# Hybrid attention block: softmax sums divided out of y^T, residual rows loaded early, six z tiles computed as Strassen pairs between the gate pairs

## The chip, the cores and the metric

The kernel runs on one core of a Trainium2 chip. The core has a matrix engine (TensorE, PE in the profile, with PEld for its weight loads), three engines for elementwise work (VectorE, DVE; ScalarE, ACT; GpSimd, POOL) and a sync engine whose queue (SP) issues all DMAs here. PE writes to PSUM, eight banks of 128 x 512 fp32. The metric is the device time of one execution in microseconds.

## The reference

One decoder block on x of 1024 rows by 1024 channels, all fp32:

```python
h = rms_norm(x, g_pre)
qa, ka, va, fa, za, qb, kb, vb, zb, gates = split(h @ w_in)
ya = fox_attention(qa, ka, va, log_sigmoid(fa + b_forget))      # 8 heads of 64, causal
ya = ya * silu(za)
yb = (softmax(q1 k1^T) - lam * softmax(q2 k2^T)) @ vb           # 4 heads of 128, rope on q, k
yb = rms_norm(yb, g_subln) * (1 - lam_init) * silu(zb)
ga, gb = split(sigmoid(gates))
merged = ga * (ya @ w_branch[0]) + gb * (yb @ w_branch[1])
out = x + rms_norm(merged @ w_out, g_post)
```

The two z projections (za and zb) together have 1024 columns: eight tiles of 128 columns, z tile 0 to 3 from za and 4 to 7 from zb. The gates have 2048 columns: eight tiles d for each of the two branches.

## The kernel before

**Arithmetic.** Every fp32 operand of a product is split into a high part and a low part (fp32r), and a product is the sum of three matmuls: high x high, high x low, low x high. A projection of one tile of 128 columns on 1024 rows, with 8 blocks of the inner dimension, is 2 row halves x 8 x 3 = 48 matmuls of 512 columns (`project`, L242 to 248). The normed input lies transposed in SBUF as hT, indexed by part (high or low), inner half kh and row half sh.

**Order.** The program is written as a sequence; a scheduler places each engine's instructions in a fixed order at compile time. Its stages are:

1. Normalize x, transpose it into hT, compute the values V (L119 to 222).
2. Attention, units u = 0 to 7 (L251 to 645). Units 0 to 3 are a differential head each, 4 to 7 two forgetting heads each. A unit's rows come in groups of two row blocks of 128. `s_row` (L410 to 431) makes one row block of softmax: scores on PE (L421, L422), bias, scale and row extreme on DVE (L423), exp on ACT with the row sum accumulated into `le` (L428), and 1/le on DVE (L430). A differential row scales p2 by -lambda/l2 on POOL (L512), p1 by 1/l1 on ACT (L514) and adds them on POOL (L515); a forgetting row is scaled by 1/l on POOL (L542). `av` (L433 to 483) then transposes the rows on PE, splits them into high and low (ACT L453, DVE L454) and multiplies with V (L474). y^T is stored to DRAM (y_d). Between the groups stand filler tasks (L623 to 644): the k and q projections of the next unit (`unit_proj`; for a differential unit with rope, whose half swaps are DMAs, L287), the z tiles that ZFILL gives to the unit (`z_tasks`, which store the projection to z_d), the sums of hT for the later Strassen products (`h_combinations`, TFILL), and the squares of y for the sub-norm (`sum_squares`, `subln_scales`, SFILL), which leave the row factors in rs_d.
3. Gates (L747 to 821). Tile d = 0 plain, d = 1 to 7 in pairs: the two branches' tiles as one 2 x 2 block product by Winograd's form of Strassen's method, seven products of 12 matmuls in place of eight (`wino`, L697 to 740; `left_operands`, L669 to 695). The sums of the weights run on POOL (L677), the splits on ACT (L664) and DVE or POOL (L665), the sums of the products on DVE (L706). The results pass a sigmoid on ACT and go to DRAM (g_d). After pair d stand the blocks `y_work(t, c)` that YORD[d] names (L762 to 772): y_t times the sub-norm factor (t < 4), times z, times sigmoid(z); z comes back from z_d. Weights for a pair are loaded into two buffers with the tag wraw; work tiles of 512 columns come from `tmp`, tag t, 8 buffers.
4. Branch products (L824 to 873): y^T is split (yT, L837, L838) into slots that the gate stage has used, then 384 matmuls (L848) and the merge with the gates into mg.
5. Output product (L876 to 970), again by Strassen pairs: `out_pair(i)` makes row blocks i and i + 4 from mg. `out_half` loads the residual half row (L931), squares (ACT, L933), multiplies by g_post (DVE L936 or POOL L939), and, when both halves of a row are there, forms the row factor on POOL (L943, L112, L113) and applies it and the residual (L948 to L951) before the store (L952). The residual tile `ox` has two buffers.

Of the kernel before, what the change touches and what calls it, by code (L numbers as in the profile page):

```python
# [46 lines left out]
def tile_hybrid_block(  # L47
# [47 lines left out]
    sub_rs = const.tile([P, 4, 8], F32, name="sub_rs")  # L95

# [8 lines left out]
    ss_d = dram.tile([4, S], F32, name="ss_d")  # L105
    rs_d = dram.tile([4, S], F32, name="rs_d")
# [144 lines left out]
    with ExitStack() as st:  # L251
# [158 lines left out]
        def s_row(T, m, i, X, bias, boff, nm):  # L410
# [16 lines left out]
            le = small.tile([P, 1], F32, tag="l", name=f"l{nm}_{m}_{i}", bufs=8)  # L427
            nc.scalar.activation(pr[:, 0:n], pr[:, 0:n], AF.Exp,  # L428
                                 bias=mx[:, len(pcs) - 1:len(pcs)], scale=-1.0, accum_out=le)
            nc.vector.reciprocal(le, le)  # L430
            return pr, le
# [53 lines left out]
        def unit_attn(u, T):  # L485
# [17 lines left out]
            if diff:  # L503
                def row(i, rows):
# [3 lines left out]
                    p1, l1 = s_row(T, 0, i, rows["X"][0], dmask, boff, f"d{u}")  # L508
                    p2, l2 = s_row(T, 1, i, rows["X"][1], dmask, boff, f"d{u}")
# [4 lines left out]
                    nc.scalar.activation(p1[:, 0:n], p1[:, 0:n], AF.Copy, scale=l1)  # L514
# [17 lines left out]
            else:  # L532
                ysb = {}

                def row(m, i, rows):
# [3 lines left out]
                    if "X" not in rows:  # L539
                        rows["X"] = swapped(T, m, i // 2, f"f{u}")  # L540
                    p1, l1 = s_row(T, m, i, rows["X"], cb[m], 0, f"f{u}")
                    nc.gpsimd.tensor_scalar(  # L542
                        p1[:, 0:n], p1[:, 0:n], l1, 1.0, op0=ALU.mult, op1=ALU.mult)
                    rows[i] = p1
# [73 lines left out]
        for u in range(8):  # L618
# [4 lines left out]
            fill = []  # L623
# [5 lines left out]
            fill[2:2] = [lambda k=k: h_combinations(k) for k in TFILL[u]]  # L629
# [15 lines left out]
        pend()  # L645

# [368 lines left out]
```

## Time and profile before

| | us |
|---|---|
| median of 3 runs | 960.3 (960.2 to 962.56) |
| the profiled execution's own time | 960.13 |
| its span in the profile | 958.0 |
| DVE busy | 627.2 |
| ACT busy | 437.0 |
| POOL busy | 489.6 |

The span is what the instructions cover; the execution's own time is 2.1 us longer. Times in a trace count from the span's start. A group's row gives the line, the engine, the operation, the tiles written and read, the count, and then busy time, mean length and the idle time of the engine before these instructions, with what released it. The chain of work that ended last is followed back from the last instruction, so an engine can be busy without being on it. Matmuls are pipelined: their printed lengths overlap, and what one costs is read from how far apart they start.

### The profile page before, as it was taken

The page shows a single profiled execution, that of the slowest core. Times are in us where ns is not written, and L with a number is a line of the kernel's source. Part 1 is how long each engine was busy: PE and PEld are TensorE (multiplying, and loading weights), DVE is VectorE, ACT ScalarE, POOL GpSimd, SP SyncE. Part 2 cuts the span into 40 slices and gives each one's busy share as a digit, 9 for nine tenths or more (in the row PEclk, how much of TensorE's full clock was granted, in tenths as well). Part 3 has the DMA queues.
Part 4 walks back from the last instruction along what each step waited for, and adds up shares of the span by engine and source line. Part 5 has one row for each costly group of instructions (what it writes and reads, how often), then busy time and mean ns, then how long its engine had stood idle before and what let it go on. Part 6 is the DMA issues. An engine that isn't in the chain of part 4 may idle for free.

```text
span 958.0 us, 13760 instructions
## 1 busy us (share of the span) xinstructions
PE 900.7 (94%) x4600; PEld 752.1 (79%) x4600; DVE 627.2 (65%) x1180; ACT 437.0 (46%) x862; POOL 489.6 (51%) x460
## 2 busy tenths in 40 slices
PE   7999989899999999999999988999999999999992
PEld 5999867787887888888878877777888768887871
DVE  7731258978768868578676478228665782559875
ACT  3521125665656574565745658323443550324331
POOL 7200035446545466464644575216655735878972
PEclk9999999999999999999999999998999989999997
DMA  9532454434334353534434350893445696210144
GB/s 314 193 110 91 142 134 114 105 80 123 97 94 138 95 155 116 154 122 130 143 123 136 103 186 28 325 377 122 139 138 172 186 370 203 73 38 1 48 150 154
DMA packets 115656, 136.95 MB, mean 143 GB/s; under 512 B 10609, under 2 KB 80241, under 8 KB 114562
## 3 DMA queue, kind: packets, MB, share of 16 engines
q1 hardware_dynamic: 115586, 136.08, 44.4%
q8 instruction: 36, 0.59, 0.3%
q14 instruction: 34, 0.28, 0.1%
HBM read 85.65 MB, written 37.81 MB: 129 GB/s over the span
## 4 chain that ended last, share of the span: by engine, by line
PE 58%; DVE 13%; POOL 8%; DMA 7%; issue 6%; ACT 5%; SPq 2%; DVEq 0%; POOLq 0%; ACTq 0%
PE x_g L713 11%; PE pv L195 9%; PE pb L848 9%; PE pz L246 7%; PE pk L246 4%; PE pq L246 3%; PE ypf L474 3%; PE pg L246 2%; PE ptf L450 2%; DMA swk<-rawk 2%; SPq L287 1%; DVE Pd L423 1%; PE ypd L474 1%; PE Sf L421 1%; DVE wo_op L890 1%
## 5 line engine op out<-in xcount | busy, mean ns | idle before, releaser
L195 PE MATMUL pv<-wvhi,hT 128*128 128x264 f32 (+2 forms) x384 | 89.3, 325 | 0.4 <-DVE hT L181 0.4
L246 PE MATMUL pk<-hT,hi_k 128*128 128x512 f32 x256 | 83.9, 401 | 4.2 <-DVE KB L298 2.4
L246 PE MATMUL pz<-hT,hi_z 128*128 128x512 f32 x256 | 85.1, 400 | 0.0
L848 PE MATMUL pb<-yT,hi_br 128*128 128x512 f32 x256 | 80.8, 398 | 1.9 <-ACT hi_br L232 1.6
L246 PE MATMUL pq<-hT,hi_q 128*128 128x512 f32 x256 | 82.3, 395 | 0.0
L713 PE MATMUL x_g<-T,a_g 128*128 128x512 f32 x336 | 79.5, 392 | 1.6 <-ACT a_g L664 1.2
L713 PE MATMUL x_o<-wo_op,a_o 128*128 128x512 f32 x336 | 77.4, 391 | 2.4 <-ACT a_o L664 1.2
L713 PEld LDWEIGHTS x_o<-wo_op,a_o 128*128 128x128 f32 x336 | 62.8, 188 | 16.9 <-ACT a_o L664 2.1
L713 PEld LDWEIGHTS x_g<-T,a_g 128*128 128x128 f32 x336 | 63.5, 190 | 15.7 <-ACT a_g L664 1.6
L195 PEld LDWEIGHTS pv<-wvhi,hT 128*128 128x128 f32 x384 | 64.6, 190 | 6.2 <-DVE hT L181 0.7
L542 POOL TENSOR_SCALAR Pf<-Pf,lf 128x1024 f32<-128x1024 f32 (+3 forms) x64 | 52.5, 824 | 30.2 <-DVE lf L430 27.4
L713 PE MATMUL x_g<-hT,a_g 128*128 128x512 f32 x252 | 62.0, 400 | 2.6 <-ACT a_g L664 2.0
L428 ACT ACTIVATE Pf<-Pf,mxf 128x1024 f32<-128x1024 f32 (+3 forms) x64 | 49.8, 778 | 32.1 <-DVE mxf L423 29.5
L428 ACT ACTIVATE Pd<-Pd,mxd 128x128 f32<-128x128 f32 (+7 forms) x64 | 49.5, 774 | 30.0 <-DVE mxd L423 28.2
L538 POOL TENSOR_TENSOR cb<-cb,trim 128x128 f32<-128x128 f32 x64 | 30.0, 470 | 62.9 <-DVE mxf L423 45.1
L195 PE MATMUL pv<-wvlo,hT 128*128 128x512 f32 (+2 forms) x192 | 61.9, 325 | 0.0
L512 POOL TENSOR_SCALAR Pd<-Pd,ld 128x128 f32<-128x128 f32 (+7 forms) x32 | 25.6, 799 | 68.8 <-DVE ld L511 38.2
L848 PEld LDWEIGHTS pb<-yT,hi_br 128*128 128x128 f32 x256 | 49.1, 193 | 13.1 <-ACT hi_br L232 2.0
L713 PEld LDWEIGHTS x_g<-hT,a_g 128*128 128x128 f32 x252 | 48.5, 193 | 13.7 <-ACT a_g L664 2.4
L246 PEld LDWEIGHTS pk<-hT,hi_k 128*128 128x128 f32 x256 | 47.6, 190 | 14.4 <-DVE KB L298 2.5
L454 DVE TENSOR_TENSOR plf<-ptf,phf 128x512 fp32r<-128x512 f32 (+1 forms) x80 | 49.6, 633 | 10.1 <-ACT phf L453 9.5
L246 PEld LDWEIGHTS pz<-hT,hi_z 128*128 128x128 f32 x256 | 47.9, 191 | 8.7
(243 smaller groups left out, 2426.6 us busy)
## 6 DMA issues: line engine op xcount, KB each, us to landing
t_d<-t SPq DMA_DIRECT2D x32, 256.0 KB, 2.2
T<-t_d SPq DMA_DIRECT2D x8, 1024.0 KB, 14.9
raw<-in_w_in_dram SPq DMA_DIRECT2D x14, 512.0 KB, 4.1
g_d<-c_g SPq DMA_DIRECT2D x21, 256.0 KB, 3.9
vb_d<-vbs SPq DMA_DIRECT2D x8, 512.0 KB
va_d<-vas SPq DMA_DIRECT2D x8, 512.0 KB, 3.8
raw_k<-in_w_in_dram SPq DMA_DIRECT2D x8, 512.0 KB, 5.3
raw_q<-in_w_in_dram SPq DMA_DIRECT2D x8, 512.0 KB
```

The source lines that it names most:

```text
L195: nc.tensor.matmul(ps[n], lhsT=hT[hp][k // 4][i // 4][:, k % 4, hs], rhs=wt[k][:, a:b], start=first, stop=(k == KT - 1 and hp == 1))
L246: nc.tensor.matmul(ps, lhsT=a[:, k, :], rhs=hT[h][k // 4][c][:, k % 4, :], start=(k == 0 and a is hi and h == 0), stop=(k == KT - 1 and a ...
L287: nc.sync.dma_start(sw[b * 32:(b + 1) * 32, :], raw[o * 32:(o + 1) * 32, :])
L428: nc.scalar.activation(pr[:, 0:n], pr[:, 0:n], AF.Exp, bias=mx[:, len(pcs) - 1:len(pcs)], scale=-1.0, accum_out=le)
L450: nc.tensor.transpose(pt[:, o * P:(o + 1) * P], rows[2 * g + r][:, j * P:(j + 1) * P], ident)
L454: nc.vector.tensor_tensor(pl[:, 0:n], pt[:, 0:n], ph[:, 0:n], op=ALU.subtract)
L474: nc.tensor.matmul(o, lhsT=a, rhs=b[:, src], start=(j == 0 and n == 0), stop=(odd == 1 and jj == g and n == len(prods) - 1))
L512: nc.gpsimd.tensor_scalar(p2[:, 0:n], p2[:, 0:n], l2, 1.0, op0=ALU.mult, op1=ALU.mult)
L538: nc.gpsimd.tensor_tensor(diag, diag, trim, op=ALU.add)
L542: nc.gpsimd.tensor_scalar(p1[:, 0:n], p1[:, 0:n], l1, 1.0, op0=ALU.mult, op1=ALU.mult)
L713: nc.tensor.matmul(x[m], lhsT=a[:, ai, k, :], rhs=right[m][bi][k], start=(k == 0 and n == 0), stop=(k == 3 and n == 2))
L848: nc.tensor.matmul(ps, lhsT=a[:, kk, :], rhs=yT[g][h][:, k % 2, sl], start=(k == 0 and a is hi and h == 0), stop=(k == 3 and a is lo))
```

## The change

- **Sums out of the rows.** The row sums are kept in a tile `lsum` and no longer divided out row by row. A forgetting row goes unscaled into the product with V. A differential row is p1 + p2 x (l1 x -lambda / l2), so it is l1 times what it was. `save_sums(u)`, a filler task of unit u + 1 (after the last unit for u = 7), transposes the sums of a unit and stores them to l_d, as 1/l for the forgetting heads and as l1 for the differential ones. The sub-norm cancels l1, with the small constant scaled by l1 squared; for the forgetting heads `y_work` multiplies y^T by 1/l, loaded from l_d as a broadcast row.
- **z tiles 0 to 5** leave the filler of the units. They are computed as three Strassen pairs (0, 1), (2, 3) and (4, 5), after the gate pairs 1, 3 and 5, and each block that comes out goes straight into `y_work` as z; z_d is used for tiles 6 and 7 alone. YORD keeps four blocks of y (t = 2 and 3). All eight y tiles are loaded ahead of gate pair 1.
- **Output.** The residual rows 2, 6, 3 and 7 are loaded, after the first two output pairs, into columns of mg that those pairs have read. The last pair's order of products is (1, 6, 5, 7, 3, 4, 2) in place of (1, 6, 5, 2, 3, 7, 4). The row factor is (sum + D x eps) to the power -1/2, with g_post scaled by sqrt(D) once; one POOL operation leaves the chain of a row.

The diff, cut to its core:

```diff
-YORD = ((), ((0, 0),), ((0, 1), (1, 0)), ((1, 1), (2, 0)), ((2, 1), (4, 0), (4, 1)),
-        ((3, 0), (5, 0), (5, 1)), ((3, 1), (6, 0), (6, 1), (7, 0), (7, 1)), ())
-ZFILL = ((0,), (1,), (), (2,), (3,), (4,), (5,), (6, 7))
+ZFILL = ((), (), (), (), (), (), (), (6, 7))
+ZPAIRS = {1: 0, 3: 2, 5: 4}
+YORD = ((), (), ((2, 0),), (), ((2, 1), (3, 0)), (), ((3, 1),), ())
...
         def subln_scales(t):
-            rs = sub_rs[:, t]
+            rs, ls = sub_rs[:, t], sub_l[:, t]
             nc.sync.dma_start(rs, ss_d[t].rearrange("(p j) -> p j", j=8))
-            rstd_of(rs, rs, P, SUB_EPS)
+            nc.sync.dma_start(ls, l_d[8 + t].rearrange("(p j) -> p j", j=8))
+            nc.gpsimd.tensor_tensor(ls, ls, ls, op=ALU.mult)
+            nc.vector.scalar_tensor_tensor(rs, ls, P * SUB_EPS, rs, op0=ALU.mult, op1=ALU.add)
+            rstd_of(rs, rs, P, 0.0)
...
+        def save_sums(u):
+
+            hs = slice(8 + u, 9 + u) if u < 4 else slice(2 * u - 8, 2 * u - 6)
+            n = 8 * (hs.stop - hs.start)
+            src = lsum[:, hs].rearrange("p h i -> p (h i)")
+            if u >= 4:
+                nc.vector.reciprocal(src, src)
+            ps = pj.tile([P, CH], F32, tag="pj", name=f"pl{u}")[0:n, 0:P]
+            nc.tensor.transpose(ps, src, ident)
+            rows = small.tile([16, P], F32, tag="lrow", name=f"lr{u}", bufs=1)
+            nc.scalar.copy(rows[0:n], ps)
+            nc.sync.dma_start(l_d[hs].rearrange("h (i p) -> (h i) p", p=P), rows[0:n])
...
-            nc.vector.reciprocal(le, le)
-            return pr, le
+            return pr
...
-                    nc.vector.tensor_tensor(l2, l2, nlam, op=ALU.mult)
+                    nc.vector.reciprocal(l2, l2)
+                    nc.vector.tensor_scalar(
+                        l2, l2, l1, nlam, op0=ALU.mult, op1=ALU.mult)
...
-                    nc.scalar.activation(p1[:, 0:n], p1[:, 0:n], AF.Copy, scale=l1)
...
-                    nc.gpsimd.tensor_scalar(
-                        p1[:, 0:n], p1[:, 0:n], l1, 1.0, op0=ALU.mult, op1=ALU.mult)
...
-            fill = []
+            fill = [lambda u=u: save_sums(u - 1)] if u else []
...
-    def y_work(t, c):
+    def y_work(t, c, zs=None):
         ys = yz[t // 2][:, t % 2, c * CH:(c + 1) * CH]
-        zs = tmp.tile([P, CH], F32, tag="t", name=f"zs{t}_{c}")
-        nc.sync.dma_start(zs, z_d[(t + 4) % 8][:, c * CH:(c + 1) * CH])
+        if zs is None:
+            zs = tmp.tile([P, CH], F32, tag="t", name=f"zs{t}_{c}")
+            nc.sync.dma_start(zs, z_d[(t + 4) % 8][:, c * CH:(c + 1) * CH])
+        rb = tmp.tile([P, CH], F32, tag="t", name=f"rb{t}_{c}")
         if t < 4:
-            rb = tmp.tile([P, CH], F32, tag="t", name=f"rb{t}_{c}")
...
+        else:
+            for m in range(2):
+                h = 2 * t - 8 + m
+                nc.sync.dma_start(
+                    rb[64 * m:64 * m + 64],
+                    l_d[h:h + 1, c * CH:(c + 1) * CH].to_broadcast([64, CH]))
+            nc.vector.tensor_tensor(ys, ys, rb, op=ALU.mult)
...
+    def z_pair(tz):
+        c0 = (ZA + tz * P) if tz < 4 else (ZB + (tz - 4) * P)
+        pair(f"z{tz}", [c0, c0 + P], ORD, lambda n, c: lambda t: y_work((tz + n + 4) % 8, c, t))
...
-    for t in range(4):
+    for t in (4, 5, 2, 3, 6, 7, 0, 1):
         y_load(t)
     for d in range(1, KT):
-        if d == 4:
-            for t in range(4, 8):
-                y_load(t)
         gates_pair(d, ORD if d < KT - 1 else (7, 5, 6, 4, 1, 2, 3))
         for t, c in YORD[d]:
             y_work(t, c)
+        if d in ZPAIRS:
+            z_pair(ZPAIRS[d])
...
+    nc.gpsimd.tensor_scalar(gp_bc, gp_bc, math.sqrt(D), 1.0, op0=ALU.mult, op1=ALU.mult)
...
+    def residual_early(i):
+
+        xs = mg[:, :, (i - 2) * P:(i - 1) * P]
+        nc.sync.dma_start(xs, x2[i * P:(i + 1) * P, :].rearrange("p (k n) -> p k n", k=KT))
+        xres[i] = xs
...
+        if not st:
+            nc.gpsimd.tensor_scalar(ss, ss, D * EPS, 0.0, op0=ALU.add, op1=ALU.add)
...
-            rstd_of(rs, rs, D, EPS)
-            for e, o, xs, _ in st:
+            nc.gpsimd.tensor_tensor(rs, rs, mhalf[:, 0:1], op=ALU.pow)
+            for n, (e, o, xs, _) in enumerate(st):
...
+    for i in (2, 6, 3, 7):
+        residual_early(i)
     run_all(out_pair(2, ORD))
-    run_all(out_pair(3, (1, 6, 5, 2, 3, 7, 4)))
+    run_all(out_pair(3, (1, 6, 5, 7, 3, 4, 2)))
```

`pair`, which `z_pair` and `gates_pair` now share, loads two weight tiles and runs `wino` as `gates_pair` did before.

More of the change, by code (lines that the diff above doesn't have):

```diff
@@ L95, in tile_hybrid_block @@
     sub_rs = const.tile([P, 4, 8], F32, name="sub_rs")
+    sub_l = const.tile([P, 4, 8], F32, name="sub_l")
+    lsum = const.tile([P, 12, 8], F32, name="lsum")
     hT = [[[hpool.tile([P, 4, CH], F32R, tag=f"h{part}{kh}{sh}", name=f"hT{part}{kh}{sh}")
@@ L105, in tile_hybrid_block @@
     ss_d = dram.tile([4, S], F32, name="ss_d")
+    l_d = dram.tile([12, S], F32, name="l_d")
     rs_d = dram.tile([4, S], F32, name="rs_d")
@@ L796, in h_load, with pair @@
             h_ops[m] = [[t[:, k, :] for k in range(4)] for t in ts]
[L798 to L807 removed]
+    def pair(nm, cols, order, out):
+        raw = []
+        for n in range(2):
+            r = wpool.tile([P, KT, P], F32, tag="wraw", name=f"raw{nm}_{n}")
+            nc.sync.dma_start(r, w_cols(cols[n]))
+            raw.append(r)
+        left = left_operands(nm, raw[0][:, 0:4], raw[0][:, 4:8], raw[1][:, 0:4], raw[1][:, 4:8])
+        run_all(wino(nm, left, h_ops, order, *(out(n, c) for n in range(2) for c in range(2))))
+    def gates_pair(d, order):
+        pair(f"g{d}", [GT + br * D + d * P for br in range(2)], order,
+             lambda br, c: lambda t: gate_out(d, br, c, t, t))
+    def z_pair(tz):
+        c0 = (ZA + tz * P) if tz < 4 else (ZB + (tz - 4) * P)
+        pair(f"z{tz}", [c0, c0 + P], ORD, lambda n, c: lambda t: y_work((tz + n + 4) % 8, c, t))
     ORD = (1, 6, 5, 7, 2, 3, 4)
```

52 lines of the change are left out of this document (23 added, 29 removed).

## The prediction

> **What bounds the kernel now.** I read the page first (share of the engines, the chain that ended last), then the view of windows, cut where the kernel's stages change, then the chain inside each window, then groups and timeline where a term needs a price.
>
> ```profile
> span 958.0 us, 13760 instructions
> ...
> PE 900.7 (94%) x4600; PEld 752.1 (79%) x4600; DVE 627.2 (65%) x1180; ACT 437.0 (46%) x862; POOL 489.6 (51%) x460
> ...
> PE 58%; DVE 13%; POOL 8%; DMA 7%; issue 6%; ACT 5%; SPq 2%; DVEq 0%; POOLq 0%; ACTq 0%
> ```
>
> ```profile
> core 0: us, PE busy (x) PEld busy (x) DVE busy (x) ACT busy (x) POOL busy (x), PEclk, DMA share, GB/s
> 145.00:309.00 164.00, 155.32 (x805) 128.46 (x804) 132.23 (x313) 99.56 (x204) 85.32 (x70) 0.99 0.40 108
> 309.00:353.00 44.00, 43.76 (x245) 37.12 (x244) 31.91 (x92) 29.28 (x65) 20.94 (x20) 1.00 0.40 118
> 353.00:561.00 208.00, 204.43 (x1153) 175.31 (x1152) 143.91 (x342) 119.97 (x252) 116.56 (x140) 1.00 0.43 132
> 561.00:603.20 42.20, 35.48 (x229) 28.75 (x227) 34.07 (x102) 31.61 (x71) 21.88 (x33) 1.00 0.22 75
> ...
> 625.30:768.40 143.10, 137.24 (x590) 111.67 (x588) 91.00 (x101) 57.42 (x98) 81.18 (x54) 0.98 0.58 187
> ...
> 939.40:958.00 18.60, 0.02 (x1) 0.00 (x0) 9.38 (x14) 3.61 (x9) 3.13 (x7) 0.62 0.38 140
> ```
>
> The page says TensorE, at 94%. But only 58% of the chain is PE, and the windows say why the average misleads. Differential attention (145 to 353 us, units 0 to 3) has DVE at 132.23 of 164.00 us, 81%, close behind PE. Forgetting attention (353 to 603) has DVE at 69% until its last 42 us, where no engine is full. The gates (625 to 768) have PE nearly solid; in the last 18.6 us PE does nothing at all. So the kernel is a row of stages, each with its own limit, and PE time taken from one and put in another isn't the same time.
>
> How much of z (silu gate projections) ends last in each window is in the chain:
>
> ```profile
> by line: issue 10.9%; DMA swk<-rawk 7.5%; DVE Pd L423 6.8%; SPq L287 6.7%; PE pz L246 5.9%; PE pk L246 5.3%; DMA swq<-rawq 4.5%; ACT Pd L428 3.6%; DVE pld L454 3.5%; POOL swq L289 3.3%; PE pq L246 3.1%; DVE rawk L288 2.9%; DVE TB L298 2.7%;
> by line: PE pz L246 25.2%; PE pk L246 12.6%; PE pq L246 12.5%; PE ypd L474 12.3%; PE ptd L450 7.3%; PE Sd L421 7.2%; PE Sd L422 6.5%; ACT Pd L428 3.8%; ACT sq L350 2.7%; issue 2.5%; ACT sq L352 2.3%; ACT Pd L514 2.2%; ACT phd L453 2.0%; DVE
> by line: PE pz L246 22.7%; PE pk L246 13.1%; PE pq L246 10.6%; PE ypf L474 9.2%; PE ptf L450 7.5%; DMA t_d<-t 4.5%; PE Sf L421 4.3%; PE Sf L422 4.1%; issue 3.4%; DVE t L371 2.2%; DMA sq<-y_d 2.0%; PE ypd L474 1.3%; DVE f L379 1.3%; ACT Pf L
> 145.00:309.00 164.00, 27.47 (x96) 18.70 (x96) 2.31 (x4) 0.99 0.40 108
> 353.00:561.00 208.00, 57.69 (x226) 41.22 (x226) 5.26 (x9) 1.00 0.43 132
> ```
>
> The first three rows are the chains of 145 to 309, 309 to 353 and 353 to 561; the last two are windows of the instructions on tile pz alone, the first number in brackets counting z matmuls. Before 309 us the chain is the rope swaps (DMA, SP), DVE and issue; z is 5.9%. After 309 it is z and the projections.
>
> **The change, part by part.**
>
> *z tiles 0 to 5 out of attention.* A tile is 48 matmuls of 512 columns. Their printed means of 400 ns overlap; the price is a dense stretch:
>
> ```profile
> 625.30 19.05 PE x_g L713 x84
> L430 DVE RECIPROCAL lf<-lf 128x1 f32<-128x1 f32 x64 | 10.2, 160 | 15.1 <-ACT Pf L428 14.7
> L430 DVE RECIPROCAL ld<-ld 128x1 f32<-128x1 f32 x64 | 9.8, 158 | 12.0 <-ACT Pd L428 11.4
> L236 DVE TENSOR_TENSOR lo_z<-raw_z,hi_z 128x1024 fp32r<-128x1024 f32 x8 | 12.2, 1528 | 3.9 <-POOL hi_z L234 3.8
> L514 ACT ACTIVATE Pd<-Pd,ld 128x128 f32<-128x128 f32 (+7 forms) x32 | 24.8, 775 | 23.7 <-DVE ld L430 23.6
> L542 POOL TENSOR_SCALAR Pf<-Pf,lf 128x1024 f32<-128x1024 f32 (+3 forms) x64 | 52.5, 824 | 30.2 <-DVE lf L430 27.4
> ```
>
> 19.05 / 84 = 0.227 us each. Six tiles are 288 matmuls, 65.4 us of PE. That is the upper price of what leaves. The lower price is z's share of the chain: 5.9% of 164 is 9.7 us for tiles 0 and 1 (x96); 25.2% of 44 is 11.1 for tile 2; 22.7% of 208 is 47.2 for 226 matmuls, of which 144 are tiles 3 to 5, so 30.1. Sum 50.9. I take the middle, **-58**, because neither row is nearer: filler on a full PE delays everything behind it, but before 309 us something else is then due.
>
> Can the others follow? Of the 458.2 us from 145 to 603, DVE is busy in 342.1 (the four rows). Six lo_z (9.2), 64 lf and 32 ld reciprocals (10.2 and 5.1) go: about 318. A wall of 397 us (458 less 61) puts DVE at 80%, what it holds now before 309 us. So DVE doesn't forbid it, but is level with PE in units 0 to 3.
>
> *Softmax sums out of the rows.* Besides the reciprocals, ACT's scaling of Pd (24.8 us) and POOL's of Pf (52.5 us) go. None of them is an engine at its limit; what counts is a shorter path from exp to transpose. The chain holds little of it (Pd L514 is 2.2% of 44 us, 1 us). From nothing to 8 us; I take **-3**, mostly in the last 42 us, where rows wait for one another. Added: eight small transposes with a copy and a DMA, a square on POOL and one DVE operation per subln_scales, and the row of 1/l multiplied into y^T: eight DVE operations of 1.2 us (the nearest, yd L772, is below) in the gate stage. I cost these at nothing: PE's work covers them there, and uncovered they are some 10 us of DVE.
>
> *Three Strassen pairs between the gates.* Each is 84 matmuls like the row above: 3 x 19.05 = **+57.2**. (Against 65.4 the algebra alone saves 8.2.) The stage now loses, between 625.30 and the end of its last product near 766.6 (758.45 plus 36 x 0.227, from the rows below), 141.3 - 7 x 19.05 = 8 us, by weights that come late. What a pair asks of the others:
>
> ```profile
> L665 DVE TENSOR_TENSOR a_g<-S_g,a_g 128x512 fp32r<-128x512 f32 x28 | 31.6, 1134 | 34.0 <-ACT a_g L664 34.0
> L706 DVE TENSOR_TENSOR cu_g<-x_g,cu_g 128x512 f32<-128x512 f32 x14 | 9.6, 684 | 6.6 <-PE x_g L713 6.4
> L772 DVE TENSOR_TENSOR yd<-yd,zs 128x512 f32<-128x512 f32 x8 | 9.8, 1223 | 2.6 <-ACT zs L771 2.4
> L770 POOL TENSOR_TENSOR yf<-yf,zs 128x512 f32<-128x512 f32 x8 | 13.9, 1741 | 0.0
> 739.89 4.72 DMA raw<-in_w_in_dram
> 758.45 8.32 PE L713 MATMUL x_g<-hT,a_g 128*128 128x512 f32 x36
> 771.51 86.94 PE pb L848 x372
> ```
>
> Five splits at 1.13, seven sums at 0.68 and, for its four blocks of y, eight products at 1.2: 20.0 us of DVE in 19.05 of PE. A gate pair has 10.4, so two in turn need 31 to 35 us of 38.1. POOL needs four sums, two splits and four products: four at 1.74 and six that I take at 1.5, some 16 us. That fits on average, with little slack inside a z pair; DVE runs in order, and a product that waits for its l_d row holds the splits behind it. The trace has a model: at 739.89 the chain runs through a weight load that came late, its buffer freed by a split on POOL that stood behind products of y. I take **+4** for three pairs, bounds 0 and 10.
>
> *The end of the gates.* Now eight of sixteen y blocks stand after pairs 5 and 6, and yT waits for them. From 766.6 to 858.45 there are 91.8 us for 384 branch matmuls, 87.2 at 0.227: 4.7 lost. Afterwards only one block follows pair 6: **-4**, bounds -4.7 and 0. The z_d writes and reads of six tiles go; DMA is at 0.58 in that stage, so I cost that at nothing.
>
> *Residual rows early, tail reordered.* In the last 18.6 us:
>
> ```profile
> 942.93 0.75 DVE L951 SCALAR_TENSOR_TENSOR cu_o<-cu_o,ors,ox 128x512 f32<-128x512 f32 x1 [3.95 <-DMA ox<-in_x_dram]
> 948.24 0.72 ACT L948 ACTIVATE go<-go,ors 128x512 f32<-128x512 f32 x1 [1.21 <-POOL ors L113]
> 949.04 1.27 POOL L949 TENSOR_TENSOR go<-go,lx 128x512 f32<-128x512 f32 x1 [0.83 <-ACT go L948]
> 951.74 0.63 ACT L933 ACTIVATE gx<-cu_o 128x512 f32<-128x512 f32 x1 [0.33 <-DVE cu_o L706]
> 952.27 0.19 ACT L933 ACTIVATION_READ_ACCUMULATOR gx<-cu_o 128x1 f32 x1
> 952.54 0.19 POOL L943 TENSOR_TENSOR ors<-oss,oss 128x1 f32<-128x1 f32 x1 [2.23 <-ACT gx L933]
> 953.09 0.55 POOL L113 TENSOR_TENSOR ors<-ors,mhalf 128x1 f32<-128x1 f32 x1
> 953.68 1.42 DVE L951 SCALAR_TENSOR_TENSOR go<-go,ors,lx 128x512 f32<-128x512 f32 x2 [1.30 <-POOL ors L113]
> ```
>
> DVE sits 3.95 us on a residual half row (row 2 or 6) of a two-buffer tile, and the last sums queue behind it. With rows 2, 3, 6 and 7 loaded into spent columns of mg, that wait goes. What is late next is the chain itself after the last product (row 3's first half): sum 0.68 (the price of cu_g above), square 0.63 + 0.19, add 0.19, power 0.55, scale 0.72, add 1.27, then the store, 2.9 (958.0 less 955.1, DVE's last end), and some 0.7 of hand-overs: 7.8 us against 18.6. Leftovers of rows 2 and 6 may stand before it: **-10**, bounds -11 and -5. The four loads wait on SP until pairs 0 and 1 have read their columns; stores of rows 0, 1, 4 and 5 can queue behind them, but none ends last.
>
> Sum: -58 - 3 + 57.2 + 4 - 4 - 10 = -13.8. Against the profiled run's 960.13 us (span 958.0 and 2.1 around it) that is 946.3; that run stands 0.2 below the median, so **946.5**. The bounds of all terms together: low -65.4 - 8 + 57.2 - 4.7 - 11 gives 928; high -50.9 + 57.2 + 10 - 5 gives 971.
>
> **A page against it.** In the gate stage between 650 and 740 us DVE's two-SBUF-input operations are stretched: the yd product above has a mean of 1223 ns, while the same kind of sum with one input from PSUM takes 684. The Trainium skill, SBUF — State Buffer, section Who interferes with whom, says a DVE instruction with two SBUF inputs and a GpSimd instruction that reads SBUF exclude each other for their whole length. By that rule the trace's stretch is waiting, and the two engines' times add.
>
> **The rivals.** *A: something other than z ends last in attention* (slower). If the rope swaps and DVE keep units 0 to 2 as long as they are, z tiles 0 and 1 filled holes and save nothing; tile 2 saves 8 and tiles 3 to 5 25, since DVE and PE come level there too: -33, no gain from the sums. -33 + 57.2 + 4 - 4 - 10 = +14: 974 us; it decides below a saving of 47 (57.2 + 4 - 4 - 10). For it: 81% DVE, and a chain before 309 us in which PE has 14%. Against: unit 3's window is a quarter z, and 15 us of DVE go with the reciprocals.
>
> *B: DVE and POOL together set the z pairs.* Unstretched, thirteen two-input DVE operations at 0.68 (8.8) and ten of POOL at 1.3 (13; L949 shows 1.27) make 21.8 us in a z pair, 2.8 over PE. Three times that, with late weights before and after each at 2 us (a quarter of the 8 now lost): 3 x (2.8 + 4) = 20 in place of 4: 962. Against: a gate pair needs only 11, so the average fits. By the Trainium skill, SBUF — State Buffer, section Who interferes with whom, the adding up is the rule wherever gate pairs can't make up for it.
>
> *C: PE stays 88% efficient.* The 2432 PE instructions of the four attention windows, each at the slot of its width (0.227 for 512 columns, less in proportion), come to about 403 us, an estimate, of 458. If the 458 shrink in proportion, z is worth 65.4 / 0.88 = 74: -74 - 3 + 57.2 + 4 - 4 - 10 = -30: 930. DVE would be at 84%.
>
> *D: the z part does nothing on balance* (saving 61 eaten by stalls), only the ends count: 960 - 4 - 10 is 946, with the stalls of three pairs 950 to 956, within the forecast's own range.
>
> **How the numbers follow.** Forecast (with D, 936 to 957): 0.57. A, 958 to 980: 0.18. B, 955 to 965: 0.12, split a quarter faster, a half same, a quarter slower. C, 925 to 936: 0.13. A measurement of this kernel can tell about 0.3%, 2.9 us: faster is below 957.4, slower above 963.2. A gives 0.15 slower, 0.03 same; forecast and C all faster: faster 0.73, same 0.09, slower 0.18. To leave out 2 in 10 the range drops the upper half of A and the lower half of C: 931 to 968.
>
> **What would show it.** Attention should end 61 us earlier (near 542), its DVE share near 80%; if the row of units 0 to 3 is still some 200 us long, A holds. The gates should take 200 us for ten pairs; gaps after z pairs, with POOL or DVE as releaser, mean B. Branch products should follow the gates within 1 us. After PE's last product 8 to 9 us should be left, with no idle of DVE on a residual. The forecast is wrong if attention saves less than 47.

## The result and the profile after

The changed kernel takes **989.3 us** (987.41 to 991.91) where the kernel before, measured beside it, takes 960.6: a ratio of 1.031 (95% interval 1.026 to 1.036). It is slower, by 29 us. The forecast was 946.5 with a range of 931 to 968.

The page of the changed kernel, header and engines:

```profile
span 990.1 us, 13549 instructions
...
PE 911.1 (92%) x4572; PEld 756.4 (76%) x4572; DVE 637.5 (64%) x1130; ACT 425.0 (43%) x850; POOL 462.3 (47%) x413
```

TensorE's share has hardly fallen (94% before), which says little; the stages say more. First the windows of the kernel before at its two halves of attention (units 0 to 3, then 4 to 7), then those of the changed kernel: the two halves (the border is the first score product of unit 4), the ten pairs between the gates, the branch products, the output products, and what is left after TensorE's last product. Columns as in the prediction.

```profile
core 0: us, PE busy (x) PEld busy (x) DVE busy (x) ACT busy (x) POOL busy (x), PEclk, DMA share, GB/s
110.40:351.60 241.20, 227.89 (x1167) 188.44 (x1166) 179.79 (x421) 134.07 (x278) 112.58 (x94) 0.99 0.41 114
351.60:603.20 251.60, 241.30 (x1388) 205.15 (x1386) 179.38 (x447) 152.98 (x325) 139.44 (x172) 1.00 0.39 122
```

```profile
111.60:339.00 227.40, 201.57 (x1007) 163.60 (x1005) 169.51 (x386) 112.99 (x245) 117.00 (x97) 0.95 0.39 106
339.00:577.40 238.40, 220.31 (x1267) 187.14 (x1267) 167.00 (x390) 148.74 (x321) 83.15 (x104) 0.96 0.39 117
...
600.90:806.20 205.30, 196.55 (x841) 160.01 (x840) 128.23 (x147) 74.21 (x125) 107.58 (x73) 0.98 0.46 142
...
806.20:893.30 87.10, 87.10 (x386) 72.10 (x385) 45.18 (x52) 22.17 (x27) 56.03 (x31) 1.00 0.51 169
893.30:975.40 82.10, 77.85 (x337) 62.39 (x335) 67.78 (x64) 28.01 (x57) 64.02 (x52) 1.00 0.28 89
...
975.40:990.10 14.70, 0.00 (x0) 0.00 (x0) 8.12 (x12) 3.61 (x9) 3.20 (x7) 0.58 0.20 77
```

They show that attention went from 241.2 + 251.6 to 227.4 + 238.4, 27 us less and not 61, and that in the new windows neither TensorE nor VectorE is full. The pairs took 62 us more. The table sums it up; a stage begins with TensorE's first instruction on its tiles.

| stage, us | before | after | difference | forecast |
|---|---|---|---|---|
| input and V | 110.4 | 111.6 | +1.2 | 0 |
| attention | 492.8 | 465.8 | -27.0 | -58 -3 |
| plain gate tile | 21.9 | 23.5 | +1.6 | 0 |
| pairs | 143.3 | 205.3 | +62.0 | +57.2 +4 |
| branch products | 91.2 | 87.0 | -4.2 | -4 |
| output products | 79.8 | 82.1 | +2.3 | 0 |
| after the last product | 18.6 | 14.7 | -3.9 | -10 |
| span | 958.0 | 990.1 | +32.1 | -13.8 |

The 32 of this one profiled run is 29 between the medians.

### The profile page after: what moved, and what is told of

Same layout as the page of the kernel before. It is cut to its first block, busy times and chain, and to the rows that moved or that the text cites. A ratio compares the mean times of both kernels' runs of the same rounds, so it can differ in the third digit from the quotient of the medians.

```text
span 990.1 us, 13549 instructions
## 1 busy us (share of the span) xinstructions
PE 911.1 (92%) x4572; PEld 756.4 (76%) x4572; DVE 637.5 (64%) x1130; ACT 425.0 (43%) x850; POOL 462.3 (47%) x413
## 5 line engine op out<-in xcount | busy, mean ns | idle before, releaser
L249 PE MATMUL pk<-hT,hi_k 128*128 128x512 f32 x256 | 88.5, 420 | 1.3 <-ACT rawk L286 1.3
L733 PE MATMUL x_g<-T,a_g 128*128 128x512 f32 x336 | 83.5, 405 | 6.4 <-ACT a_g L684 4.8
L249 PE MATMUL pq<-hT,hi_q 128*128 128x512 f32 x256 | 85.3, 400 | 0.0
L733 PE MATMUL x_g<-hT,a_g 128*128 128x512 f32 x252 | 59.2, 389 | 0.0
L249 PEld LDWEIGHTS pk<-hT,hi_k 128*128 128x128 f32 x256 | 50.4, 203 | 11.1 <-issue 1.7
L446 ACT ACTIVATE Pf<-Pf,mxf 128x1024 f32<-128x1024 f32 (+4 forms) x64 | 49.7, 777 | 21.2 <-DVE mxf L442 20.8
L467 PE MATMUL ptf<-ident,Pf 128*128 128x128 f32 x288 | 46.6, 285 | 9.3 <-DVE plf L471 9.0
L249 PE MATMUL pk<-hT,lo_k 128*128 128x512 f32 x128 | 53.0, 414 | 2.0 <-DVE lo_k L239 2.0
L249 PEld LDWEIGHTS pq<-hT,hi_q 128*128 128x128 f32 x256 | 47.9, 191 | 8.9
L685 DVE TENSOR_TENSOR a_g<-S_g,a_g 128x512 fp32r<-128x512 f32 x28 | 27.3, 976 | 40.0 <-ACT a_g L684 39.9
```

The costliest lines, as they stand in the source:

```text
L249: nc.tensor.matmul(ps, lhsT=a[:, k, :], rhs=hT[h][k // 4][c][:, k % 4, :], start=(k == 0 and a is hi and h == 0), stop=(k == KT - 1 and a ...
L446: nc.scalar.activation(pr[:, 0:n], pr[:, 0:n], AF.Exp, bias=mx[:, len(pcs) - 1:len(pcs)], scale=-1.0, accum_out=le)
L467: nc.tensor.transpose(pt[:, o * P:(o + 1) * P], rows[2 * g + r][:, j * P:(j + 1) * P], ident)
L685: eng.tensor_tensor(lo, src, hi, op=ALU.subtract)
L733: nc.tensor.matmul(x[m], lhsT=a[:, ai, k, :], rhs=right[m][bi][k], start=(k == 0 and n == 0), stop=(k == 3 and n == 2))
```

## The experiments

### One part at a time

First each part alone. The z part:

```diff
 # before
+ZPAIRS = {1: 0, 3: 2, 5: 4}     # z tiles 0 to 5 in pairs; ZFILL and YORD as in the change
 # rows, y_work's factor and output as before
```

> The kernel before with only the z part: tiles 0 to 5 leave the units and come back as three pairs between the gate pairs; sums and output as before. Theory 1 (the rows of attention are paced by DVE and its neighbours, z was filler in holes): attention again ends only some 20 to 28 us earlier than 603, the gates grow by 58, so 990 to 998 us. Theory 2 (the sums part made attention longer and ate what z's leaving gave): attention ends near 545 and the time is 950 to 960.

Measured: 981.5 us, ratio 1.023 (1.019 to 1.027). Attention is 464.8, the pairs 198.3, the branch products 87.0. That is below the 990 to 998 of theory 1, but its two parts are as that theory had them, and the whole loss but 7 us is here: the pairs cost 55.0 (198.3 less 143.3), attention gives back 28.0.

The sums, and the tail:

```diff
 # before
+sums kept in lsum, save_sums, 1/l in y_work   # sums_only
 # before
+residual_early, order (1, 6, 5, 7, 3, 4, 2), sqrt(D) in g_post   # tail_only
 # both: sums_tail
```

> The kernel before with only the sums divided out of y^T; z stays filler, the output stage as before. Theory 1: 952 to 960 us, since 15 us of DVE reciprocals go and rows wait less. Theory 2: 980 us or more.

> The kernel before with only the new output stage (early residual rows, row factor, last order). In the trace of the changed kernel 14.8 us are left after PE's last product against 18.6, and the output products take 2.4 us longer. If both belong to this part: 957 to 960 us. If the longer products come from elsewhere (another placing of the whole program): 955 to 957. The forecast's -10 would be 950.

> The changed kernel with z tiles 0 to 5 back in the units and no z pairs: sums and output stage new. Theory 1: the sum of the two parts, 950 to 958 us, some 35 us below the changed kernel. Theory 2: 975 us or more.

Measured: the sums alone 967.4, ratio 1.009 (1.007 to 1.012); the tail alone 955.8, ratio 0.996 (0.994 to 0.998); both 968.0, ratio 1.009 (1.006 to 1.012). Neither theory had 967 or 968 for the kernels with the sums. The three parts added up, 22 + 8 - 3.5, are 27 of the 29; but sums and tail together are no faster than the sums alone, where adding up would give 964, so "additive" holds to some 4 us only. The sums shortened nothing: attention was 494.7 with them, 492.8 without. They cost 7.2 us in the pairs (150.5 against 143.3). The part that was costed at nothing lost more than the tail gained.

### Where the sums lose

The wait view of VectorE in the pairs' window of the kernel with the sums alone, and a stretch of its chain there (start, length, what):

```profile
DVE yf L798 <- DMA rb<-l_d: 6.7, 8, 1.8
```

```profile
733.24 3.23 DMA rb<-l_d
...
736.56 1.73 DVE yf L798
...
740.65 1.31 POOL yf L799
...
743.68 1.30 POOL a_g L686
744.98 0.02 issue
745.00 4.26 DMA rawg<-in_w_in_dram
```

It is the pattern that the prediction had quoted from the kernel before, with a new head: the row of 1/l takes 3.23 us to come, the product on VectorE waits for it, GpSimd's product with z behind that, then the split of a gate pair on GpSimd, whose weight buffer comes free late, so that the next weights are loaded late. Two kernels tell the row of 1/l (its load and the work tile that it takes) from the operation:

```diff
 # sums alone, without the rows of 1/l (the forgetting heads stay undivided)
-nc.sync.dma_start(rb[64 * m:64 * m + 64], l_d[...].to_broadcast([64, CH]))
-nc.vector.tensor_tensor(ys, ys, rb, op=ALU.mult)
+nc.vector.tensor_tensor(ys, ys, ys, op=ALU.max)      # sums_noload: an operation of the same size
+                                                     # sums_nomult: none
```

> The sums-only kernel without the loads of 1/l in the gate stage: the multiplication of the forgetting heads' y^T is replaced by an operation of the same shape on y^T alone, so the output lacks the division for these heads. If the wait for the load costs the 7 us by which its gate stage is longer than before (150.5 against 143.3), the stage is back at 143 to 146. If it is DVE's eight more operations, it stays at 149 to 151.

> The sums-only kernel without loads and without the eight operations (the forgetting heads are left undivided). Both theories: gate stage 142 to 144, as before; the difference to the run without loads is what the eight DVE operations cost by themselves.

Measured: 961.4, ratio 1.003 (1.000 to 1.005), and 960.6, ratio 1.002 (0.999 to 1.004). The pairs take 142.0 and 141.0 where they took 150.5: in these traces the row is worth 8.5 us and the eight operations 1. Between the medians the row is worth 6, and the step from one of the two kernels to the other is within the noise.

### What makes the holes in attention

To see what z's 65 us had been, I took the start times of all of TensorE's matmuls and set each against the slot of its width, as the prediction did. What a matmul starts late by more than 0.15 us is a hole; those at half pace (last section) are left out of it. The count depends on how a change of width is treated, so a figure is good to some 4 us. The first two rows of this table, which goes on with the experiments below, carry the answer:

| | units 0-3, us | holes | units 4-7, us | holes |
|---|---|---|---|---|
| before | 241.2 | 17.9 | 251.6 | 15.1 |
| after | 227.4 | 34.1 | 238.4 | 25.9 |
| spread_even | 233.1 | 40.5 | 233.8 | 26.5 |
| dve_relief | 233.5 | 37.8 | 231.9 | 24.8 |
| v1_pp8 | 224.2 | 30.2 | 232.4 | 25.1 |
| rows_light | 224.9 | 33.0 | 218.3 | 13.8 |
| rows_nopool | 211.1 | 18.3 | 228.4 | 22.9 |
| rows_bare | 202.1 | 13.4 | 217.9 | 17.0 |

65 us of matmuls left, 27 us of holes came, and the other 11 us that attention did not give back are matmuls at half pace (some 7) and delays too short to count: z had kept TensorE busy while rows were on their way. In the changed kernel full and hollow stretches follow one another; windows of 20 us each:

```profile
200.00:220.00 20.00, 19.87 (x112) 17.06 (x111) 15.81 (x34) 11.88 (x28) 7.52 (x8) 1.00 0.19 49
220.00:240.00 20.00, 14.93 (x75) 11.19 (x74) 19.15 (x47) 11.56 (x24) 10.96 (x10) 0.93 0.62 168
...
420.00:440.00 20.00, 20.00 (x113) 17.26 (x112) 12.51 (x25) 9.98 (x20) 2.67 (x5) 1.00 0.32 93
440.00:460.00 20.00, 17.34 (x104) 14.13 (x102) 18.55 (x42) 14.71 (x35) 11.24 (x15) 0.91 0.46 117
```

TensorE is full while the next unit's projections last and VectorE is then at 12 to 16 of 20; when they are used up VectorE is at 19 and TensorE waits. The kernel before has fewer hollow stretches (160 to 180 us, with TensorE at 15.87 and VectorE at 18.75, is one), and none at 440 us:

```profile
420.00:440.00 20.00, 20.00 (x109) 17.19 (x108) 15.52 (x36) 10.94 (x25) 10.12 (x14) 1.00 0.45 153
440.00:460.00 20.00, 20.00 (x114) 17.40 (x112) 15.77 (x44) 10.78 (x22) 9.54 (x14) 1.00 0.53 151
```

My first theory was that the projections stand badly. First their places in the sequence, with empty tasks where z was; at the same time VectorE's load:

```diff
 # null_places: after, with the projections' places as if z were in the units
+fill += [lambda: None] * NULLS[u]
 # dve_relief: after, with the weights' low parts and rope's cosine product on GpSimd
-box[kind] = load_w(f"{kind}{u}", w_cols(c0))
+box[kind] = load_w(f"{kind}{u}", w_cols(c0), False, True)
-nc.vector.tensor_tensor(raw, raw, cosT[:, sl], op=ALU.mult)
+nc.gpsimd.tensor_tensor(raw, raw, cosT[:, sl], op=ALU.mult)
```

> The changed kernel with the projections of the next unit (and the sums of hT) at the very places among a unit's rows that they had while z stood behind them: empty tasks count where z's two halves were, and the sums are saved outside the count. If attention stays long because the projections slid to later places (place theory), its 466 us fall by 10 or more and the time to 979 or less. If the rows themselves set the pace once nothing else fills PE (pace theory), within 3 us of the changed kernel's 989.

> The changed kernel with DVE work of the attention stage given to GpSimd, which is 43% busy there: the low parts of the k and q weights (16 operations, 22 us of DVE) and the cosine products of rope (16, some 15 us). If DVE's busy time sets the stretches in which PE is hollow, attention's 466 us fall by 15 or more, to a time near 970. If it is the round trip of a row (score, extreme, exp, transpose, split) and not DVE's load, it changes by less than 5 us, or gets worse where GpSimd's longer operations stand in the path to the projections.

Measured: 988.4, ratio 1.031 (1.027 to 1.035), and 989.6, ratio 1.032 (1.029 to 1.035). Attention stays at 467.8 and 465.4. The second made VectorE's busy time 17 us shorter (337 to 320) and GpSimd's 56 longer (200 to 256), and moved nothing. The first proved little: in the compiled order of TensorE the projections still stood together at a unit's beginning, since the scheduler moves them there. So the places were forced:

```diff
+tasks = [mk(kind, c, ..., n) for c in range(2) for kind in "kq" for n in range(4)]   # 6 matmuls each
+for r in rws:
+    r()
+    while nf < len(fill) and nf < len(fill) * done / (2 * len(groups) - 1):
+        with tc.issue_after(last[0].ins):      # TensorE: behind this row's last score product
+            fill[nf]()
```

> The changed kernel, with each projection of the next unit cut into four pieces of six matmuls (two inner blocks each), one or two pieces after each softmax row, and each piece tied on TensorE behind the last score product of that row, so that the compiler can no longer move the projections to the unit's beginning. Nothing is left out. My theory now (the filler's place): with z gone, the projections are issued in bulk as soon as the unit begins, and the rest of the unit has nothing to put into the holes of the rows; then this refills the hollow stretches, TensorE's excess over its slots in attention falls from 96 us to that of before (60), attention from 466 to about 430, and the time from 989 to 950 to 958. Rival 1 (the row's own trip through DVE, ACT and POOL sets the pace, wherever the projections stand): attention stays at 466 within 5 and the time within 6 of 989. Rival 2 (end of a unit): the projections now end so late that the next unit's first rows wait for them, 5 to 10 us in each of seven units; attention 470 to 500, time 995 to 1030.

> The kernel before with the three z pairs, the new tail and the spread projections, without the part on the sums. Nothing is left out. Filler's place: 8 us below the kernel with spread projections and sums, so 942 to 950, faster than both kernels. Rival 1 (row's trip): 981.5 less the tail's 4, 977. Rival 2 (end of a unit): 985 to 1020.

> The kernel before with the new tail and the spread projections, z still in the units (four pieces of a projection in turn with the two halves of a z tile). Nothing is left out. It tells whether the spreading does something of its own, with all the filler there: filler's place says little, 950 to 956 against 955.8 with the tail alone; if the end of a unit costs (rival 2), 970 or more; if spreading helps the rows in any case, 930 to 945.

Measured: 989.6, ratio 1.033 (1.029 to 1.036); 977.6, ratio 1.020 (1.017 to 1.023); 972.2, ratio 1.015 (1.012 to 1.018). Now the projections do stand between the rows, and attention is 466.9: rival 1, as it stood in the expectation, and the filler's place falls. The second is what rival 1 said to a microsecond (977). In the third, with z still there, the fixed order costs 16 us, so the scheduler's order was the better one. Its 972 is also what rival 2 named (970 or more), and in the first kernel TensorE waits 5.2 us for a unit's late projections, so a gain of the places of a few us could hide behind the cost of forcing them. But its waits in front of the differential score products, for VectorE, hardly changed (11.9 us against 12.7), and the holes did not become fewer. The holes come wherever the filler stands: that points to the rows themselves, which the next kernels test.

Then the way of a row: VectorE's step, and the number of rows in work.

```diff
 # rows_light: after; the low parts of the transposed rows are left out of the products
-nc.vector.tensor_tensor(pl[:, 0:n], pt[:, 0:n], ph[:, 0:n], op=ALU.subtract)
+pl = plz                        # one tile of zeros
 # v1: after, values of a unit in one buffer; v1_pp8: also eight row tiles
-pp = st.enter_context(tc.tile_pool(name="pp", bufs=6))
+pp = st.enter_context(tc.tile_pool(name="pp", bufs=8))
```

> The changed kernel, in which the low parts of the transposed rows are left out: one tile of zeros, written once, stands in their place in every product with V, so that TensorE does the same instructions, while VectorE loses 120 subtractions of some 0.65 us (about 78 us) and the way of a row from its transpose to its product no longer runs through VectorE. If VectorE's part of a row makes the holes (theory: with z gone, the rows go at the pace of VectorE, by its load or by its step in the way), TensorE's holes in attention fall from 71 us to 40 or less, attention from 466 to 425 to 440, the time to 950 to 965. If the rows go at the pace of something else (their buffers, ScalarE, the way of a row before its transpose), attention stays within 10 of 466 and the time is 980 or more.

> The changed kernel with one buffer for the values of a unit in place of two, which frees 8 KB of each partition; nothing is left out. It is the control for the next run: the values of a unit are loaded only when the last unit has used its own, so 0 to 30 us more than 989.

> As the control, with eight buffers for the softmax rows in place of six. If the number of rows in work sets the pace (a differential group needs four tiles, so a second group can't be begun), attention is 15 us or more below that of the control; if VectorE's part or the way of a row does, it is within 5 of it.

Measured: 972.1, ratio 1.017 (1.012 to 1.023); 985.2, ratio 1.030 (1.026 to 1.034); 980.0, ratio 1.024 (1.021 to 1.027). The time of the first lies between its two expectations (its four runs spread from 966 to 977, and the trace is of the fastest), and its halves say why (window view, units 0 to 3 and 4 to 7):

```profile
111.40:336.30 224.90, 202.07 (x1013) 164.08 (x1012) 153.95 (x352) 112.91 (x246) 117.44 (x97) 0.95 0.39 107
336.30:554.60 218.30, 208.69 (x1263) 181.22 (x1261) 121.44 (x303) 147.11 (x323) 88.09 (x106) 0.99 0.43 132
```

The forgetting units went from 238.4 to 218.3 and their holes from 25.9 to 13.8, fewer than with z; the differential units stayed. I had expected the control to be up to 30 us slower than the changed kernel; it was not. Two more row tiles gave 5.6 us of attention (462.2 to 456.6), far from the 15 that would have made them the cause. For the differential units GpSimd's step was left, the scaling and adding of the second softmax:

```diff
 # rows_nopool: after; the first softmax alone goes on. rows_bare: this and rows_light
-nc.gpsimd.tensor_scalar(p2[:, 0:n], p2[:, 0:n], l2, 1.0, op0=ALU.mult, op1=ALU.mult)
-nc.gpsimd.tensor_tensor(p1[:, 0:n], p1[:, 0:n], p2[:, 0:n], op=ALU.add)
```

> The changed kernel, in which GpSimd's two operations on a differential row are left out (the scaling of the second softmax and its addition to the first, 71 us of GpSimd in units 0 to 3), so that the first softmax alone goes on and the second row's tile comes free after its exponential. All of TensorE's, VectorE's and ScalarE's instructions stay. If GpSimd's step in a row sets the pace of the differential units, their part of attention (111.6 to 339, 227.4 us, 34 us of it holes of TensorE) loses 15 us or more; if not, it stays within 5. The forgetting units stay at 238 in either case.

> Both left out: GpSimd's two operations on a differential row, and VectorE's low parts of the transposed rows (a tile of zeros in their place). If the rest of the holes in the differential units is one way of a row through GpSimd and VectorE together, they fall to below 15 us there, as they did in the forgetting units without the low parts (25.9 to 13.8), and attention goes to 415 to 430; if they stay at 30, neither engine sets the pace there, and what is left is the way from the scores to the exponential or the projections with their rope.

Measured: 963.3, ratio 1.005 (1.002 to 1.008), and 946.7, ratio 0.987 (0.978 to 0.997), the latter from two runs only, 943.2 and 950.3. The windows of the first, then of the second (the trace of the 943.2):

```profile
111.50:322.60 211.10, 197.37 (x1035) 165.44 (x1034) 155.58 (x388) 112.89 (x248) 45.52 (x37) 0.97 0.42 113
322.60:551.00 228.40, 213.07 (x1241) 182.07 (x1240) 165.49 (x386) 147.78 (x319) 75.39 (x100) 0.98 0.41 124
```

```profile
111.10:313.10 202.00, 191.96 (x1036) 162.46 (x1035) 136.92 (x353) 113.32 (x248) 45.90 (x36) 0.98 0.43 118
313.10:531.00 217.90, 205.28 (x1240) 178.53 (x1238) 120.30 (x302) 145.33 (x320) 82.33 (x102) 0.99 0.43 133
```

Units 0 to 3 go from 227.4 to 211.1 and their holes from 34.1 to 18.3, the level of before; with both steps gone attention is 419.9, 73 us below the kernel before, which has both and needs both. So two steps of a row make most of the holes that came, each mainly in its own half: **GpSimd's scaling and adding in the differential units, VectorE's low parts in the forgetting ones.** Without GpSimd's operations VectorE is busy for 14 us less there too (169.51 to 155.58, last section), but that isn't the cause: without the low parts it is busy for 16 us less in the same units (153.95), and they take 224.9 against 227.4. In the forgetting units it isn't told apart whether VectorE's load or its place in the way of a row counts. (Units 4 to 7 also lost 10 us in the first of the two. The halves overlap: the last products of unit 3's rows end at 371 us in the changed kernel, 32 behind the border, and at 341, 19 behind it, without GpSimd's step.) In the views of the changed kernel GpSimd's step shows only weakly. First TensorE's waits in attention (total us, times, longest), then the group of VectorE's score step:

```profile
PE Sd L440 <- DVE mxd L442: 12.7, 12, 2.7
PE ptf L467 <- DVE plf L471: 9.0, 6, 4.1
PE ptd L467 <- POOL Pd L536: 2.9, 5, 1.4
```

```profile
L442 DVE CUSTOM_DVE_ANT_0 Pd<-Sd,dmask 128x512 f32<-128x512 f32 (+3 forms) x64 | 35.8, 568 | 15.3 <-POOL Pd L536 10.1 <-PE Sd L441 3.6 <-PE ptd L467 1.1
```

The first row names VectorE, but behind it stands GpSimd: of VectorE's 15.3 us idle before that step 10.1 were spent on a row tile that GpSimd still had.

### The tail

The end of the changed kernel in its timeline (start, length, engine, line, what, and in brackets the idle time before it and what ended that):

```profile
966.80 0.56 POOL L990 TENSOR_TENSOR ors<-ors,mhalf 128x1 f32<-128x1 f32 x1
...
967.40 3.47 DVE L998 SCALAR_TENSOR_TENSOR c_o<-c_o,ors,mg 128x512 f32<-128x512 f32 x2 [3.00 <-POOL ors L990]
...
971.58 1.74 DVE L998 SCALAR_TENSOR_TENSOR c_o<-c_o,ors,mg 128x512 f32<-128x512 f32 x1 [0.71 <-POOL ors L990]
972.83 2.56 PE L733 MATMUL x_o<-wo_op,a_o 128*128 128x512 f32 x10 [1.14 <-POOL a_o L685]
...
973.91 0.68 DVE L726 TENSOR_TENSOR cu_o<-x_o,c_o 128x512 f32<-128x512 f32 x1
```

The wait for a residual is gone, but the last steps of rows 2 and 6 still stand ahead of the last pair's sums in VectorE's order, now waiting for the row factor, which stands behind products with g_post and, for row 6, a split in GpSimd's. The first sum of the pair starts at 973.91 though its products were ready several us earlier. So these four steps were put behind sums that don't wait:

```diff
 # tail_only; the last steps of rows 2 and 6 are kept and issued between pair 3's products
+for n, _ in enumerate(out_pair(3, (1, 6, 5, 7, 3, 4, 2))):
+    if n in (3, 4):
+        with tc.issue_after(lastadd[0].ins):     # VectorE: behind the last sum so far
+            finish(*later.pop(0))
```

> The kernel before with the new tail, in which the last steps of rows 2 and 6 on VectorE are issued behind the sums of the last output pair's fourth and fifth product, where they no longer wait for the row factor on GpSimd. Nothing is left out. If the wait of 3.0 and 0.7 us at the head of VectorE's queue is what kept the tail from its forecast, what is left after TensorE's last product falls from 15.0 to 11 to 12 and the time from 955.8 to 952; if GpSimd's queue (splits and factors) sets the end, it stays at 15 and 956.

Measured: **948.9 us, ratio 0.991 (0.988 to 0.994)**, the fastest of the kernels here that leave nothing out: it is 0.9% below the kernel before, and the ratio's interval lies just below that of the tail alone. Its timeline at the same place, and the window after TensorE's last product:

```profile
927.97 0.69 DVE L708 TENSOR_TENSOR cu_o<-x_o,c_o 128x512 f32<-128x512 f32 x1 [1.32 <-ACT c_o L718]
928.76 0.69 DVE L708 TENSOR_TENSOR c_o<-x_o,cu_o 128x512 f32<-128x512 f32 x1
...
930.89 2.44 DVE L948 SCALAR_TENSOR_TENSOR c_o<-c_o,ors,mg 128x512 f32<-128x512 f32 x2
```

```profile
937.60:947.00 9.40, 0.03 (x1) 0.00 (x0) 4.48 (x7) 2.17 (x5) 3.39 (x5) 0.77 0.32 122
```

VectorE sums while GpSimd makes the factor, and 9.4 us are left where the tail alone left 15.0. That is a larger gain than the 11 to 12 expected: VectorE has 7 operations left in this window where the changed kernel had 12 in its own, so the wait had also held up sums and products with g_post, and what follows them.

## Why the prediction was wrong

**The step that failed is "z tiles 0 to 5 out of attention", -58 with bounds -50.9 and -65.4.** It gave 27 (28 alone). Its lower price was taken from z's share of the chain of waits. That share tells how much of the way that ended last ran over z in the order that was there; it doesn't bound what is saved when z goes, because the next-latest way may be barely shorter. Here it was: the rows' way through GpSimd and VectorE. The check that should have caught it, VectorE at 80% of a 397 us wall "doesn't forbid it", was an average over stretches: within them VectorE is at 12 or at 19 of 20 us, and rows go back and forth between four engines. Rival A's condition (attention saves less than 47) came true. It left 8 us to units 0 to 2 and 25 to tiles 3 to 5; the differential units gave 14 and the forgetting ones 13, with the z part alone 8 and 20, in a trace in which some 11 us more of matmuls stand before the border. So the places can't be judged sharply by the halves. In the cause it had VectorE and the rope swaps where the runs show GpSimd in the differential units. With 974 it was still 15 us too good.

**Sums, -3, and their added operations at nothing.** Both wrong. The rows got no shorter (+1.9 alone); that neither the reciprocals nor the scalings that left were the late step is my reading, which no run tests by itself. The additions cost 7: the cover I named, TensorE's work, is none where a load stands at the head of VectorE's queue in a stage that runs on late weights. The forecast had the model of it (the chain at 739.89), and had written that a product that waits for its l_d row holds the splits behind it, but priced it within the +4 of the z pairs.

**Three pairs, +57.2 and +4 of stalls.** The forecast of 61.2 meets the 62.0, but by luck in part: the z pairs alone cost 55.0, so their stalls of 4 didn't come, and the sums' 7, costed at nothing, filled the place. Rival B falls. Its mechanism is there, but costs nothing on balance; in the pairs' window of the kernel with the z pairs alone:

```profile
L706 DVE TENSOR_TENSOR c_g<-x_g,cu_g 128x512 f32<-128x512 f32 x12 | 8.2, 683 | 2.1 <-PE x_g L713 2.0
...
L773 DVE TENSOR_TENSOR yf<-yf,c_z 128x512 f32<-128x512 f32 x6 | 7.2, 1194 | 2.8 <-ACT c_z L772 2.6
```

Sums with one input from PSUM still take 683 ns and products with both inputs from SBUF 1194, yet TensorE is busy 193.14 us of 198.40 there.

**End of the gates, -4.** Right: 91.2 to 87.0, and the window 806.20 to 893.30 is solid.

**Tail, -10, bounds -11 and -5.** It gave 3.9, and the output products took 2.3 more; TensorE's waits for GpSimd's splits are 3.0 us there and were 1.1 before. The chain I added up, 7.8 us, was the right one: in the last kernel it takes 8.3 from its sum to the end and begins 1.1 after TensorE's last product. The clause "leftovers of rows 2 and 6 may stand before it" named what came, and was given no price. With the order mended the tail is 9.4, close to the 8 to 9 that the text expected.

**Rivals C and D** fall with the saving. The chances: 0.18 for slower was too little for a term whose lower end was no bound.

## What to carry to other kernels

An instruction's share of the chain of waits is not what its removal saves: look for the next-latest way, and see whether the matmuls to be moved are filler, by counting TensorE's holes beside full stretches. In a stage where an in-order engine feeds everything, a small load at the head of its queue holds up all that stands behind it (eight waits of 6.7 us together, 6 to 8.5 us of the whole), and a step that waits belongs behind those that don't; the new tail with that reordering, without the z pairs and the sums, beat both kernels.

## What the runs showed of the hardware

**Matmuls at half pace after a hollow stretch.** In the changed kernel's timeline:

```profile
235.03 0.34 PE L441 MATMUL Sd<-KB,X1d 128*128 128x384 f32 x1
236.92 0.66 PE L440 MATMUL Sd<-KA,TA 128*128 128x512 f32 x1 [1.55 <-DVE mxd L442]
237.38 0.63 PE L441 MATMUL Sd<-KA,X0d 128*128 128x512 f32 x1
237.81 0.63 PE L440 MATMUL Sd<-KA,TA 128*128 128x512 f32 x1
238.23 0.63 PE L441 MATMUL Sd<-KA,X0d 128*128 128x512 f32 x1
```

They start 0.42 to 0.46 us apart in place of 0.227. The granted clock is 0.93 in the window 220 to 240 above, and 0.53 in the 3.6 us that begin with these matmuls; in the 3.4 us before them it is 1.00, with TensorE busy for 1.85 (window view):

```profile
233.70:237.10 3.40, 1.85 (x10) 1.34 (x10) 3.40 (x8) 1.53 (x4) 2.00 (x2) 1.00 0.51 123
237.00:240.60 3.60, 3.60 (x10) 2.53 (x10) 3.54 (x11) 3.41 (x6) 0.95 (x1) 0.53 0.53 145
```

Counted over the kernel, 78 matmuls of 512 columns start 0.38 to 0.47 us apart, against 41 before: at 0.2 us each, some 7 us of the loss is this and not waiting. The Trainium skill, TensorE: Matmul & The Clock Gate, section Part 1: The HAM clock gate, says that TensorE goes to half its clock after an idle window of about 3.4 us; the halving agrees, but the idle times in front of the matmuls shown are 1.55 us and less.

**GpSimd stretches VectorE's operations with two inputs from SBUF.** Rope's addition in units 0 to 3, in the changed kernel and then with GpSimd's two row operations left out:

```profile
L293 DVE TENSOR_TENSOR rawk<-rawk,swk 128x512 f32<-128x512 f32 x8 | 10.3, 1293 | 3.6 <-POOL swk L292 3.5
```

```profile
L293 DVE TENSOR_TENSOR rawk<-rawk,swk 128x512 f32<-128x512 f32 x8 | 5.5, 688 | 3.4 <-POOL swk L292 3.3
```

The same operation falls from 1293 to 688 ns, and VectorE's busy time in these units from 169.51 to 155.58 us with 386 and 388 instructions. That agrees with the Trainium skill, SBUF — State Buffer, section Who interferes with whom, which has the two exclude each other. So a step that is moved to GpSimd can lengthen those that stay. In the relief above 37 us of operations left VectorE, but its busy time fell by 17: the subtractions that make TB's low part from two inputs in SBUF rose from 855 to 1930 ns, while those with one input in PSUM stayed at 693.
